# Two-layer transformer trunk on one core: the sum of squares at stage boundaries, the residual adds, and one compression weight move between engines

## The chip, the cores and the metric

The kernel runs on one core of a Trainium2 chip. The core has a matrix engine (TensorE, PE in the profile, with PEld for its weight loads), VectorE (DVE), ScalarE (ACT), GpSimd (POOL) and SyncE (SP, which here only issues DMAs); each works through its own instruction list in order and waits on semaphores for the others. The metric is the device time of one execution in microseconds.

## The reference

Two layers over 512 tokens of width 1024, in fp32. Cut to the stages:

```python
hn = rms_norm(x, norm_g[0])
parts = split_columns(hn @ w_in)                 # 8 NSA query heads, K/V x3, gates, 4 stick-breaking heads, 2 merge gates
kc = compress_blocks(k_c, cmp_pe[0], cmp_w1[0], cmp_w2[0])   # gelu(blocks @ w1) @ w2, for keys
vc = compress_blocks(v_c, cmp_pe[1], cmp_w1[1], cmp_w2[1])   # and for values
y_nsa = nsa_attention(...) @ w_nsa_o             # compressed + selected + window branches
y_sb  = stick_breaking_attention(...) @ w_sb_o
mixed = (gate_a * y_nsa + gate_b * y_sb) @ w_out
x = x + rms_norm(mixed, norm_g[1])               # boundary: post-norm, residual
hf = rms_norm(x, norm_g[2])                      #           and the next pre-norm
ff = square(relu(hf @ w_ff1)) @ w_ff2
x = x + rms_norm(ff, norm_g[3])                  # the second boundary of the layer
```

`rms_norm` divides each token by the root of the mean of its 1024 squares.

## The kernel before

Activations lie transposed, features on the 128 partitions and the 512 tokens along the free axis, so x is eight tiles x0 to x7 of 128 x 512, and a matmul of a 128 x 128 weight block moves 512 or 256 columns. Full fp32 precision comes from three matmuls in a fast fp32 format: operands are split into a high and a low part (`w_hi`, `w_lo` of a weight; `ah`, `al` of an activation), and `three` (L185 to L187) issues hi x hi, hi x lo, lo x hi.

**Weights.** The class `Weight` loads 128 x 1024 raw values into one of two buffers (tag `wr`), lets ACT copy them rounded into `w_hi` (L157), and then has POOL subtract for `w_lo` (L162). The raw buffer is free for the next load when that subtract is done. With `sub="dma"` it goes another way: ACT writes the rounded raw weight, negated, into `w_lo` (L159), and POOL issues a DMA that adds the raw weight from DRAM to it (L160); POOL then does no arithmetic on it. Which of the four first-layer weights (u = 0 to 3) of the two compressions use this is set by bits of `PLAN["CKM"]` (keys) and `PLAN["CVM"]` (values). `CKM` 2 means u = 1 of the keys.

**Boundaries.** `tail` is called four times, at the ends of `w_out` and of `w_ff2` in both layers. It handles the last five of the eight output tiles and the passage into the next stage; the last call has no next stage (`nxt` is None), so three of the four are boundaries as meant here: 1 (near 430 us), 2 (near 800) and 3 (near 1230). The 512 tokens are handled in two halves of 256. PE computes the five tiles of the first half, then those of the second. Each finished tile is copied out of PSUM by DVE (L261; at the end of `w_ff2` it is added to an earlier part, L263), ACT squares it and DVE adds the square to a running sum (`macc` after `w_out`, `facc` after `w_ff2`, L237). `rstd_fin` sums that over the partitions by a matmul with a matrix of ones (tile `ss`, L212) and forms the reciprocal root `Rpost`. `residual` then takes each of the eight tiles: `pn` = tile x gain x Rpost (DVE, L291), x = pn + x_old (POOL, L292), `ah` = rounded x times the next gain (ACT, L226), `al` = the rest (DVE, L227). PE meanwhile runs the next stage's first four column groups (`head_step`, tile `head`) over these: two k steps on the first half before the second half's `ss`, six after it, and then the second half.

**Order.** PE's list is written out by hand. The lists of the other engines are laid out by a scheduler that simulates the timeline when the kernel is built, so an edit in one place can move instructions in others. Small squares, the cosine and sine tables and `x_old` share six buffers (tag `sig`).

Of the kernel before, what the change touches and what calls it, by code (L numbers as in the profile page):

```python
# [11 lines left out]
AF = mybir.ActivationFunctionType  # L12
ALU = mybir.AluOpType
# [9 lines left out]
}  # L23
GN = 5
# [25 lines left out]
def layer_kernel(ctx, tc, xT, pos, gvec, tri, consts, smalls, w_in, w1, w_o, w_out, ff1, ff2, out):  # L50
    nc = tc.nc
    V, S, G, E = nc.vector, nc.scalar, nc.gpsimd, nc.tensor
# [9 lines left out]
    def big(tag, name, dt=F32):  # L62
        return sp.tile([P, T], dt, tag=tag, bufs=BUFS[tag], name=name)

    def half(name):
        return sp.tile([P, 256], F32, tag="sv", bufs=3, name=name)

    def psum(tag, name):
        return pp.tile([P, T], F32, tag=tag, bufs=2, name=name)
# [10 lines left out]
    x = [big("L", f"x{k}") for k in range(KT)]  # L80
# [8 lines left out]
    ones = cp.tile([P, P], F32, name="ones")  # L89
# [99 lines left out]
    def dense(ps, w, acts, k0=0):  # L189
        n = len(acts)  # L190
        for k in range(n):
            three(ps, w, k0 + k, acts[k], k == 0, k == n - 1)

    HALVES = (slice(0, 256), slice(256, 512))
    FULL = (slice(0, 512),)

    def cols(acts, c):
        return [(h[:, c], l[:, c]) for h, l in acts]

    def head_step(group, acts, c, ks):  # L200
        for k in ks:
            for ps, w in group:
                three(ps[:, c], w, k, (acts[k][0][:, c], acts[k][1][:, c]), k == 0, k == KT - 1)

    def gcol(l, n, k):
        c = (l * 4 + n) * KT + k
        return gv[:, c:c + 1]

    def rstd_fin(R, acc, c, more=None, tag="t"):
        n = c.stop - c.start  # L210
        ss = psum(tag, "ss")[:, 0:n]
        E.matmul(ss, ones, acc, start=True, stop=more is None)  # L212
        if more is not None:
            E.matmul(ss, ones, more, start=False, stop=True)
        v = half("var")
        y = R[:, c]
        S.activation(y, ss, AF.Ln, scale=1.0 / D, bias=eps_c)
        V.tensor_scalar(v, ss, 1.0 / D, EPS, ALU.mult, ALU.add)
        S.activation(y, y, AF.Exp, scale=-0.5)
        V.tensor_tensor(acc, y, y, ALU.mult)  # L220
        V.scalar_tensor_tensor(v, acc, -0.5, v, ALU.mult, ALU.mult)
        V.scalar_tensor_tensor(y, v, 1.5, y, ALU.add, ALU.mult)

    def xsplit(act, xk, g, c):
        h, l = act[0][:, c], act[1][:, c]
        S.activation(h, xk[:, c], AF.Copy, scale=g)  # L226
        V.scalar_tensor_tensor(l, xk[:, c], g, h.bitcast(F32), ALU.mult, ALU.subtract)  # L227

    def sq_add(acc, src, first, c, eng):
        n = c.stop - c.start  # L230
        if first:
            S.activation(acc, src, AF.Square)
        else:
            for o in range(0, n, 256):
                sq = sp.tile([P, 256], F32, tag="sq", bufs=2, name="sq")
                S.activation(sq, src[:, o:o + 256], AF.Square)
                eng.tensor_tensor(acc[:, o:o + 256], acc[:, o:o + 256], sq, ALU.add)  # L237

    def new_acts():
        return [(big("act", f"ah{k}", F32R), big("act", f"al{k}", F32R)) for k in range(KT)]  # L240

    def tail(l, n, mixed, acc, load, acts, prev, src, nxt, head):


        group = range(KT - GN, KT)
        last_sq = []
        na = new_acts() if nxt is not None else None
        R = big("R", "Rpost")
        R2 = big("R", "Rpre") if nxt is not None else None
        ws = [load(m, ("f", "w", "w", "w", "pt")[i]) for i, m in enumerate(group)]  # L250
        pst = [psum(("d", "s", "o", "o", "s")[i], f"tail{m}") for i, m in enumerate(group)]

        def products(hf, i):
            c = HALVES[hf]
            dense(pst[i][:, c], ws[i], cols(acts, c))

        def evacuate(hf, i):
            c = HALVES[hf]
            m, ps = group[i], pst[i][:, c]
            if prev is None:  # L260
                V.tensor_copy(mixed[m][:, c], ps)  # L261
            else:
                V.tensor_tensor(mixed[m][:, c], ps, prev[m][:, c], ALU.add)  # L263
            if nxt is None and (hf, i) == (1, GN - 1):
                last_sq.append(half("last_sq"))
                S.activation(last_sq[0], mixed[m][:, c], AF.Square)
            else:
                sq_add(acc[:, c], ps if prev is None else mixed[m][:, c], False, c, V)
            if nxt is None and hf == 1:
                S.activation(mixed[m][:, c], mixed[m][:, c], AF.Copy, scale=gcol(l, n, m))  # L270

        def old(hf):
            if src is None:
                return [x[k][:, HALVES[hf]] for k in range(KT)]
            r = []
            for j in range(4):
                t = big("sig", "x_old").rearrange("p (a t) -> p a t", a=2)
                nc.sync.dma_start(t, src[:, 2 * j:2 * j + 2, HALVES[hf]])
                r += [t[:, 0, :], t[:, 1, :]]
            return r  # L280

        def residual(hf, xo):
            c = HALVES[hf]
            for k in range(KT):
                t = big("t", "pn")[:, 0:256]
                if nxt is None and hf == 1:
                    e = G if k in ENDP else V
                    e.tensor_tensor(t, mixed[k][:, c], R[:, c], ALU.mult)
                    (G if k == 5 else e).tensor_tensor(x[k][:, c], t, xo[k], ALU.add)
                else:  # L290
                    V.scalar_tensor_tensor(t, mixed[k][:, c], gcol(l, n, k), R[:, c], ALU.mult, ALU.mult)  # L291
                    (V if nxt is None and k in (1, 4, 7) else G).tensor_tensor(x[k][:, c], t, xo[k], ALU.add)  # L292
                if nxt is not None:
                    xsplit(na[k], x[k], gcol(nxt[0], nxt[1], k), c)
                else:
                    nc.sync.dma_start(out[:, k, c], x[k][:, c])

        def squares(hf):
            c = HALVES[hf]
            acc2 = half("acc2")  # L300
            for k in range(KT):
                sq_add(acc2, x[k][:, c], k == 0, c, V)
            return acc2

        for i in range(GN):
            products(0, i)
            evacuate(0, i)
        xo = old(0)
        if src is not None:
            for k in range(KT):  # L310
                x[k] = big("L", f"x{k}")
        products(1, 0)
        rstd_fin(R, acc[:, HALVES[0]], HALVES[0])
        evacuate(1, 0)
        hd = head.start() if nxt is not None else None
        residual(0, xo)
        for i in range(1, GN):
            products(1, i)
            evacuate(1, i)
        xo = old(1)  # L320
        if nxt is None:
            for m in range(KT - GN):
                S.activation(mixed[m][:, HALVES[1]], mixed[m][:, HALVES[1]], AF.Copy, scale=gcol(l, n, m))
            rstd_fin(R, acc[:, HALVES[1]], HALVES[1], last_sq[0])
            residual(1, xo)
            return None
        head_step(hd, na, HALVES[0], (0, 1))
        rstd_fin(R, acc[:, HALVES[1]], HALVES[1])
        residual(1, xo)
        a2 = squares(0), squares(1)  # L330
        head_step(hd, na, HALVES[0], range(2, KT))
        head_step(hd, na, HALVES[1], range(PLAN["HS"]))
        rstd_fin(R2, a2[0], HALVES[0])
        head_step(hd, na, HALVES[1], range(PLAN["HS"], PLAN["HS2"]))
        rstd_fin(R2, a2[1], HALVES[1])
        head_step(hd, na, HALVES[1], range(PLAN["HS2"], KT))
        return na, R2, hd
# [118 lines left out]
    class Head:  # L456
# [5 lines left out]
        def load(self, sub=None, between=None):  # L462
            u = len(self.ws)
            self.ws.append(Weight(self.src[u], "P" if u < 3 else "w", sub, between))
# [549 lines left out]
    with tc.manual_schedule(engines={mybir.EngineType.PE}):  # L1014
        acts = new_acts()
        R = big("R", "R0")
        acc = big("st", "acc0")
# [16 lines left out]
        nxt = acts, R, hd  # L1034
        for l in range(DEPTH):
            nxt = layer(l, *nxt)
# [71 lines left out]
```

## Time and profile before

| | |
|---|---|
| three runs | 1608.31, 1613.12, 1613.18 us; median 1613.12 |
| profiled execution | 1610.72 us, span 1608.8 us |
| PE busy | 1528.3 us, 95% of the span |
| DVE, ACT, POOL busy | 858.1 (53%), 748.9 (47%), 763.2 us (47%) |
| POOL, the subtract L162 | 204 times, 2425 ns each |
| ACT, w_hi L157 | 226 times, 1059 ns each |
| raw weight loads | 3.5 to 3.7 us from issue to landing |

The profile is of one execution. A timeline row gives start and duration in us, engine, line, operation, output and inputs with the shape, how many in a row are put together (x), and in brackets how long the engine stood idle before and which engine's operation ended that. In a timeline the ends of matmuls are modelled; their starts tell the pace. PEclk is the granted clock of PE as a share of 2.4 GHz.

### The profile page before, as it was taken

The page shows a single profiled execution, that of the slowest core. Times are in us where ns is not written, and L with a number is a line of the kernel's source. Part 1 is how long each engine was busy: PE and PEld are TensorE (multiplying, and loading weights), DVE is VectorE, ACT ScalarE, POOL GpSimd, SP SyncE. Part 2 cuts the span into 40 slices and gives each one's busy share as a digit, 9 for nine tenths or more (in the row PEclk, how much of TensorE's full clock was granted, in tenths as well). Part 3 has the DMA queues.
Part 4 walks back from the last instruction along what each step waited for, and adds up shares of the span by engine and source line. Part 5 has one row for each costly group of instructions (what it writes and reads, how often), then busy time and mean ns, then how long its engine had stood idle before and what let it go on. Part 6 is the DMA issues. An engine that isn't in the chain of part 4 may idle for free.

```text
span 1608.8 us, 20693 instructions
## 1 busy us (share of the span) xinstructions
PE 1528.3 (95%) x7810; PEld 1288.8 (80%) x7810; DVE 858.1 (53%) x1495; ACT 748.9 (47%) x1379; POOL 763.2 (47%) x527
## 2 busy tenths in 40 slices
PE   7789999999989999999988899999998999999996
PEld 5667778887978888888976787788878988888886
DVE  6788854355583232314698887534447713232245
ACT  6567754553352322324446777554444523232342
POOL 4574344535544444446546724444464444444452
PEclk9899999999999999999999999999999999999998
DMA  6443312224313233233334512122342132323321
GB/s 195 121 131 92 64 55 77 66 91 145 105 43 104 93 94 103 92 102 121 117 100 131 136 49 66 53 79 71 113 144 92 47 98 92 105 92 97 100 92 53
DMA packets 49331, 153.74 MB, mean 96 GB/s; under 512 B 5952, under 2 KB 12496, under 8 KB 49232
## 3 DMA queue, kind: packets, MB, share of 16 engines
q1 hardware_dynamic: 45888, 140.84, 27.2%
q0 software_dynamic: 3200, 11.55, 4.1%
q8 instruction: 61, 1.00, 0.3%
q14 instruction: 38, 0.31, 0.1%
q10 hardware_dynamic: 144, 0.03, 0.0%
HBM read 148.15 MB, written 4.26 MB: 95 GB/s over the span
## 4 chain that ended last, share of the span: by engine, by line
PE 78%; DVE 12%; ACT 2%; issue 2%; DMA 1%; POOL 1%; DVEq 0%; ACTq 0%; POOLq 0%
PE ff L186 12%; PE ff L187 12%; PE ff L185 12%; PE proj L479 5%; PE proj L483 5%; PE proj L481 5%; PE tail L187 2%; PE tail L186 2%; PE tail L185 2%; PE y L185 2%; PE p_t L720 2%; DVE P L690 2%; PE y L186 2%; PE y L187 2%; DVE pn L291 2%
## 5 line engine op out<-in xcount | busy, mean ns | idle before, releaser
L162 POOL TENSOR_TENSOR w_lo<-w_raw,w_hi 128x1024 fp32r<-128x1024 f32 x204 | 494.6, 2425 | 506.1 <-ACT w_hi L157 493.6
L157 ACT ACTIVATE w_hi<-w_raw 128x1024 fp32r<-128x1024 f32 x226 | 239.1, 1059 | 521.2 <-PE ff L186 371.7
L483 PE MATMUL proj<-ah,w_lo 128*128 128x512 f32 x496 | 198.7, 401 | 1.7 <-POOL w_lo L162 1.7
L479 PE MATMUL proj<-ah,w_hi 128*128 128x512 f32 x496 | 199.2, 402 | 0.9 <-ACT w_hi L157 0.9
L481 PE MATMUL proj<-al,w_hi 128*128 128x512 f32 x496 | 198.9, 401 | 0.0
L185 PE MATMUL ff<-ah,w_hi 128*128 128x512 f32 x448 | 174.3, 389 | 0.0
L186 PE MATMUL ff<-al,w_hi 128*128 128x512 f32 x448 | 174.3, 389 | 0.0
L187 PE MATMUL ff<-ah,w_lo 128*128 128x512 f32 x448 | 174.3, 389 | 0.0
L186 PE MATMUL ff<-hl,w_hi 128*128 128x512 f32 x432 | 168.2, 389 | 0.7 <-DVE hl L181 0.7
L185 PE MATMUL ff<-hh,w_hi 128*128 128x512 f32 x432 | 168.1, 389 | 0.0
L187 PE MATMUL ff<-hh,w_lo 128*128 128x512 f32 x432 | 168.1, 389 | 0.0
L181 DVE TENSOR_TENSOR hl<-relu,hh 128x512 fp32r<-128x512 f32 x64 | 106.8, 1673 | 83.7 <-ACT hh L180 83.5
L483 PEld LDWEIGHTS proj<-ah,w_lo 128*128 128x128 f32 x496 | 94.8, 191 | 19.0 <-POOL w_lo L162 2.1
L479 PEld LDWEIGHTS proj<-ah,w_hi 128*128 128x128 f32 x496 | 95.0, 192 | 17.4 <-ACT w_hi L157 1.1
L481 PEld LDWEIGHTS proj<-al,w_hi 128*128 128x128 f32 x496 | 95.0, 192 | 16.7
L1003 DVE TENSOR_TENSOR ffa<-ff,ffa 128x512 f32<-128x512 f32 x38 | 26.3, 692 | 151.3 <-PE ff L187 151.3
L185 PEld LDWEIGHTS ff<-ah,w_hi 128*128 128x128 f32 x448 | 84.1, 188 | 17.5
L187 PEld LDWEIGHTS ff<-ah,w_lo 128*128 128x128 f32 x448 | 84.1, 188 | 17.3
L186 PEld LDWEIGHTS ff<-al,w_hi 128*128 128x128 f32 x448 | 84.1, 188 | 17.3
L186 PEld LDWEIGHTS ff<-hl,w_hi 128*128 128x128 f32 x432 | 81.1, 188 | 17.9 <-DVE hl L181 1.1
L185 PEld LDWEIGHTS ff<-hh,w_hi 128*128 128x128 f32 x432 | 81.1, 188 | 17.0
L187 PEld LDWEIGHTS ff<-hh,w_lo 128*128 128x128 f32 x432 | 81.1, 188 | 16.6
(311 smaller groups left out, 3401.3 us busy)
## 6 DMA issues: line engine op xcount, KB each, us to landing
w_raw<-in_ff_dram SPq DMA_DIRECT2D x128, 512.0 KB, 3.5
w_raw<-in_w_in_dram SPq DMA_DIRECT2D x69, 512.0 KB, 3.6
w_lo<-in_w_in_dram POOLq DMA_DIRECT2D x18, 512.0 KB, 7.7
w_raw<-in_w_dram SPq DMA_DIRECT2D x16, 512.0 KB, 3.6
w_raw<-in_w_o_dram SPq DMA_DIRECT2D x16, 512.0 KB, 3.5
w_raw<-in_w_out_dram SPq DMA_DIRECT2D x16, 512.0 KB, 3.7
x<-in_xT_dram SPq DMA_DIRECT2D x8, 256.0 KB, 6.8
w_lo<-in_w_dram POOLq DMA_DIRECT2D x4, 512.0 KB, 7.0
```

Of the source, the lines that this page charges most:

```text
L157: S.activation(h, raw, AF.Copy)
L162: (sub or G).tensor_tensor(l, raw, h.bitcast(F32), ALU.subtract)
L181: V.tensor_tensor(lo, src, hi.bitcast(F32), ALU.subtract)
L185: E.matmul(ps, w.hi(k), ah, start=first, stop=False)
L186: E.matmul(ps, w.hi(k), al, start=False, stop=False)
L187: return E.matmul(ps, w.lo(k), ah, start=False, stop=last)
L291: V.scalar_tensor_tensor(t, mixed[k][:, c], gcol(l, n, k), R[:, c], ALU.mult, ALU.mult)
L479: E.matmul(ps, w.hi(k), ah, start=(k == 0), stop=False)
L481: E.matmul(ps, w.hi(k), al, start=False, stop=False)
L483: E.matmul(ps, w.lo(k), ah, start=False, stop=(k == KT - 1))
L690: V.tensor_scalar(pr[h], pr[h], sm4[:, h:h + 1], None, ALU.mult)
L720: E.transpose(pt[:, P * h:P * h + P], pend[j][0][h][:, P * kt:P * kt + P], ident)
```

## The change

Three things are edited. In the three boundaries, the second half's five squares are written by ACT into tiles of their own (`sq2`, halves of three `sig` buffers), from PSUM or, at boundary 2, from the summed tile; DVE no longer adds them up, and `rstd_fin` passes them to PE, which adds five more ones-matmuls to the one over the running sum (L214, now in a loop). In `residual`, the adds x = pn + x_old at these boundaries, sixteen at each, are given to DVE where POOL did them. `CKM` becomes 0, so the low part of the keys' u = 1 weight is made by POOL's subtract as for the other weights. Lines of the changed kernel from `tail` on are numbered five higher.

```diff
--- before.py
+++ after.py
@@ -18,7 +18,7 @@
     "GE": 7, "GA": 1, "GB": 4,
     "F0": 76, "F2": 5, "F3": 1, "F1": 7, "AH": 7, "BU": 2, "QD": 77, "FS0": 4, "FS1": 4, "FE": 5, "FN00": 5, "FN01": 3, "FN02": 4,
     "FN03": 7, "FN10": 6, "FN11": 4, "FN12": 4, "FN13": 7, "FNC0": 1, "FNC1": 7, "CK0": 11, "CK1": 24, "CK2": 13,
-    "CK3": 36, "CV0": 13, "CV1": 28, "SC3": 1, "SC2": 2, "R1": 3, "R2": 4, "CKV": 1, "CKM": 2, "CVM": 1, "ORD": 2, "HS": 6, "H0": 2, "HS2": 7, "FQ": 12,
+    "CK3": 36, "CV0": 13, "CV1": 28, "SC3": 1, "SC2": 2, "R1": 3, "R2": 4, "CKV": 1, "CKM": 0, "CVM": 1, "ORD": 2, "HS": 6, "H0": 2, "HS2": 7, "FQ": 12,
     "CD": 0, "GT": 24,
 }
 GN = 5
@@ -210,8 +210,8 @@
         n = c.stop - c.start
         ss = psum(tag, "ss")[:, 0:n]
         E.matmul(ss, ones, acc, start=True, stop=more is None)
-        if more is not None:
-            E.matmul(ss, ones, more, start=False, stop=True)
+        for i, m in enumerate(more or ()):
+            E.matmul(ss, ones, m, start=False, stop=i == len(more) - 1)
         v = half("var")
         y = R[:, c]
         S.activation(y, ss, AF.Ln, scale=1.0 / D, bias=eps_c)
@@ -243,7 +243,7 @@
 
 
         group = range(KT - GN, KT)
-        last_sq = []
+        last_sq, pairs = [], []
         na = new_acts() if nxt is not None else None
         R = big("R", "Rpost")
         R2 = big("R", "Rpre") if nxt is not None else None
@@ -264,6 +264,11 @@
             if nxt is None and (hf, i) == (1, GN - 1):
                 last_sq.append(half("last_sq"))
                 S.activation(last_sq[0], mixed[m][:, c], AF.Square)
+            elif nxt is not None and hf == 1:
+                if i % 2 == 0:
+                    pairs.append(big("sig", "sq2"))
+                last_sq.append(pairs[-1][:, 256 * (i % 2) : 256 * (i % 2) + 256])
+                S.activation(last_sq[-1], ps if prev is None else mixed[m][:, c], AF.Square)
             else:
                 sq_add(acc[:, c], ps if prev is None else mixed[m][:, c], False, c, V)
             if nxt is None and hf == 1:
@@ -289,7 +294,7 @@
                     (G if k == 5 else e).tensor_tensor(x[k][:, c], t, xo[k], ALU.add)
                 else:
                     V.scalar_tensor_tensor(t, mixed[k][:, c], gcol(l, n, k), R[:, c], ALU.mult, ALU.mult)
-                    (V if nxt is None and k in (1, 4, 7) else G).tensor_tensor(x[k][:, c], t, xo[k], ALU.add)
+                    (G if nxt is None and k not in (1, 4, 7) else V).tensor_tensor(x[k][:, c], t, xo[k], ALU.add)
                 if nxt is not None:
                     xsplit(na[k], x[k], gcol(nxt[0], nxt[1], k), c)
                 else:
@@ -321,11 +326,11 @@
         if nxt is None:
             for m in range(KT - GN):
                 S.activation(mixed[m][:, HALVES[1]], mixed[m][:, HALVES[1]], AF.Copy, scale=gcol(l, n, m))
-            rstd_fin(R, acc[:, HALVES[1]], HALVES[1], last_sq[0])
+            rstd_fin(R, acc[:, HALVES[1]], HALVES[1], last_sq)
             residual(1, xo)
             return None
         head_step(hd, na, HALVES[0], (0, 1))
-        rstd_fin(R, acc[:, HALVES[1]], HALVES[1])
+        rstd_fin(R, acc[:, HALVES[1]], HALVES[1], last_sq)
         residual(1, xo)
         a2 = squares(0), squares(1)
         head_step(hd, na, HALVES[0], range(2, KT))
```

The order of DVE at boundary 1 shows the first two edits. Before, from the first half's Rpost on (`pn`, `al` with their tile numbers; `mix` is a tile of the stage's output, `macc` the running sum):

```order
L291 SCALAR_TENSOR_TENSOR pn_4177<-mix0_3765,gv_67,Rpost_3929 128x256
L291 SCALAR_TENSOR_TENSOR pn_4182<-mix1_3766,gv_67,Rpost_3929 128x256
L291 SCALAR_TENSOR_TENSOR pn_4187<-mix2_3767,gv_67,Rpost_3929 128x256
L291 SCALAR_TENSOR_TENSOR pn_4192<-mix3_3768,gv_67,Rpost_3929 128x256
L237 TENSOR_TENSOR macc_3773<-macc_3773,sq_4242 128x256
L291 SCALAR_TENSOR_TENSOR pn_4197<-mix4_3769,gv_67,Rpost_3929 128x256
L227 SCALAR_TENSOR_TENSOR al0_3914<-x0_4122,gv_67,ah0_3913 128x256
L261 COPY mix5_3770<-tail5_3971 128x256
L237 TENSOR_TENSOR macc_3773<-macc_3773,sq_4270 128x256
L291 SCALAR_TENSOR_TENSOR pn_4202<-mix5_3770,gv_67,Rpost_3929 128x256
L261 COPY mix6_3771<-tail6_3972 128x256
L227 SCALAR_TENSOR_TENSOR al1_3916<-x1_4123,gv_67,ah1_3915 128x256
```

And in the changed kernel, from the same place, where `x0` to `x5` are the adds now on DVE:

```order
L296 SCALAR_TENSOR_TENSOR pn_4175<-mix0_3764,gv_67,Rpost_3928 128x256
L296 SCALAR_TENSOR_TENSOR pn_4180<-mix1_3765,gv_67,Rpost_3928 128x256
L296 SCALAR_TENSOR_TENSOR pn_4185<-mix2_3766,gv_67,Rpost_3928 128x256
L296 SCALAR_TENSOR_TENSOR pn_4190<-mix3_3767,gv_67,Rpost_3928 128x256
L261 COPY mix4_3768<-tail4_3969 128x256
L297 TENSOR_TENSOR x0_4121<-pn_4175,x_old_4113 128x256
L297 TENSOR_TENSOR x1_4122<-pn_4180,x_old_4113 128x256
L297 TENSOR_TENSOR x2_4123<-pn_4185,x_old_4115 128x256
L297 TENSOR_TENSOR x3_4124<-pn_4190,x_old_4115 128x256
L296 SCALAR_TENSOR_TENSOR pn_4195<-mix4_3768,gv_67,Rpost_3928 128x256
L261 COPY mix5_3769<-tail5_3970 128x256
L296 SCALAR_TENSOR_TENSOR pn_4200<-mix5_3769,gv_67,Rpost_3928 128x256
```

The two adds into macc are gone from this stretch, four x adds stand behind the first four pn, and al0 stands behind pn5; al1 follows six rows later (al0, pn6, pn7, x4, x5, al1).

On ACT at boundary 1, the second half's last squares in the changed kernel (`sq2`, read from the PSUM tiles `tail6` and `tail7`):

```order
L226 ACTIVATE ah4_3920<-x4_4125,gv_67 128x256
L271 ACTIVATE sq2_4266<-tail6_3971 128x256
L226 ACTIVATE ah5_3922<-x5_4126,gv_67 128x256
L226 ACTIVATE ah6_3924<-x6_4127,gv_67 128x256
L226 ACTIVATE ah7_3926<-x7_4128,gv_67 128x256
L271 ACTIVATE sq2_4319<-tail7_3972 128x256
L217 ACTIVATE Rpost_3928<-ss_4353,eps_c_78 128x256
```

The last of the five squares stands behind ah7 and right ahead of Rpost's first step.

On ACT in layer 1 (q and K rows of the sparse attention; the `w_hi` here is that of the next projection), before:

```order
L571 ACTIVATE qph_7509<-q_7495 128x512
L531 ACTIVATE K1w_7444<-kr_7469 64x512 x2
L533 ACTIVATE K2s_7445<-K2s_7445 64x512
L157 ACTIVATE w_hi_7636<-w_raw_7634 128x1024
L350 ACTIVATE xr10_7503<-qr_7497 64x512
L350 ACTIVATE xr11_7506<-qr_7497 64x512
L543 ACTIVATE V20_7447<-v_t_7513 128x4x64
```

and in the changed kernel:

```order
L576 ACTIVATE qph_7504<-q_7490 128x512
L536 ACTIVATE K1w_7439<-kr_7464 64x512 x2
L538 ACTIVATE K2s_7440<-K2s_7440 64x512
L355 ACTIVATE xr10_7498<-qr_7492 64x512
L355 ACTIVATE xr11_7501<-qr_7492 64x512
L548 ACTIVATE V20_7442<-v_t_7508 128x4x64
L157 ACTIVATE w_hi_7630<-w_raw_7628 128x1024
```

The w_hi has moved behind the two xr and a V. On POOL, the subtract for the keys' u = 1 weight stands in layer 0 exactly where the DMA stood, between `qr` and `qpl`; in layer 1 it stands ahead of `qr` and the block splits `bhl`, where the DMA stood behind `qr`.

## Rows read from the trace of the kernel before

**Rows 1.** Waits of PE: engine, line, what ended them; us in total, times, longest.
```profile
PE ss L212 <- DVE macc L237: 8.2, 2, 4.1
...
PE ss L212 <- DVE facc L237: 5.7, 2, 5.0
```

**Rows 2.** Timeline of PE, boundary 1: start, us, operation [wait before it <-releaser].
```profile
428.83 0.60 PE L212 MATMUL ss<-macc,ones 128*128 128x256 f32 x2
...
429.38 0.28 PE L186 MATMUL tail<-ml,w_hi 128*128 128x256 f32 x1
...
444.39 0.39 PE L186 MATMUL head<-al,w_hi 128*128 128x256 f32 x1 [1.90 <-DVE al L227]
...
450.08 1.22 PE L212 MATMUL ss<-macc,ones 128*128 128x256 f32 x2 [4.12 <-DVE macc L237]
```

**Rows 3.** Windows behind the sums: length; busy us of PE, PEld, DVE, ACT, POOL; PEclk; DMA.
```profile
450.10:453.60 3.50, 3.50 (x14) 3.32 (x15) 2.63 (x7) 2.83 (x8) 0.24 (x1) 0.50 0.60 191
453.70:458.00 4.30, 4.30 (x38) 4.30 (x38) 4.30 (x9) 2.32 (x6) 2.78 (x4) 1.00 0.01 1
809.70:815.40 5.70, 5.70 (x25) 5.52 (x26) 5.16 (x13) 3.41 (x10) 0.95 (x2) 0.50 0.15 57
```

**Rows 4.** Timeline of PE, boundary 2.
```profile
809.66 1.22 PE L212 MATMUL ss<-facc,ones 128*128 128x256 f32 x2 [4.95 <-DVE facc L237]
```

**Rows 5.** Timeline of DVE, boundary 1.
```profile
431.56 0.43 DVE L222 SCALAR_TENSOR_TENSOR Rpost<-var,Rpost 128x256 f32<-128x256 f32 x1
...
447.14 0.41 DVE L261 COPY mix<-tail 128x256 f32<-128x256 f32 x1
447.47 2.23 DVE L227 SCALAR_TENSOR_TENSOR al<-x,gv,ah 128x256 fp32r<-128x256 f32 x1
449.62 0.41 DVE L237 TENSOR_TENSOR macc<-macc,sq 128x256 f32<-128x256 f32 x1
```

**Rows 6.** Timeline of POOL, boundary 1.
```profile
436.66 3.55 POOL L292 TENSOR_TENSOR x<-pn,x_old 128x256 f32<-128x256 f32 x4
...
446.89 2.52 POOL L162 TENSOR_TENSOR w_lo<-w_raw,w_hi 128x1024 fp32r<-128x1024 f32 x1
```

**Rows 7.** Timeline of PE, compression of keys in layer 0.
```profile
67.71 0.47 PE L379 MATMUL cmp_h<-w_lo,bhl 128*64 128x256 f32 x1 [8.83 <-DMA w_lo<-in_w_dram]
```

**Rows 8.** Windows from the next w_lo to cmp_o, layers 0 and 1 (columns as in 3).
```profile
63.24:96.21 32.97, 22.43 (x107) 18.00 (x108) 22.36 (x43) 19.25 (x38) 23.72 (x14) 0.86 0.51 141
858.03:890.55 32.52, 24.78 (x100) 19.22 (x100) 27.33 (x44) 21.09 (x42) 24.09 (x14) 0.84 0.44 129
```

**Rows 9.** Timeline of PE, the same stretch of layer 1.
```profile
860.45 0.80 PE L483 MATMUL proj<-ah,w_lo 128*128 128x512 f32 x1 [1.71 <-POOL w_lo L162]
...
890.55 0.64 PE L409 MATMUL cmp_o<-cmp_ht,sml 128*64 128x32 f32 x4 [2.89 <-DVE cmp_ht L400]
```

**Rows 10.** Timeline of ACT, layer 0.
```profile
57.20 1.06 ACT L157 ACTIVATE w_hi<-w_raw 128x1024 fp32r<-128x1024 f32 x1
...
60.40 1.28 ACT L350 ACTIVATE xr<-qr 64x512 fp32r<-64x512 f32 x2
...
62.11 1.06 ACT L157 ACTIVATE w_hi<-w_raw 128x1024 fp32r<-128x1024 f32 x1
```

**Rows 11.** Timeline of POOL, layer 0.
```profile
60.09 1.58 POOL L143 TENSOR_TENSOR qpl<-q,qph 128x512 fp32r<-128x512 f32 x1
```

**Rows 12.** Timeline of DVE, layer 0.
```profile
46.11 3.88 DVE L344 TENSOR_TENSOR rope_sh<-rope_sh,sinT 128x512 f32<-128x512 f32 x1
...
58.82 0.69 DVE L344 TENSOR_TENSOR rope_sh<-rope_sh,sinT 128x512 f32<-128x512 f32 x1
```

**Rows 13.** Timeline of ACT, layer 1.
```profile
844.46 1.04 ACT L157 ACTIVATE w_hi<-w_raw 128x1024 fp32r<-128x1024 f32 x1
...
856.90 1.06 ACT L157 ACTIVATE w_hi<-w_raw 128x1024 fp32r<-128x1024 f32 x1
```

**Rows 14.** Timeline of POOL, layer 1.
```profile
849.94 0.86 POOL L160 DMA_DIRECT2D w_lo<-in_w_dram  x1
```

## Prediction

> **What bounds the kernel now.** I read first the busy shares: TensorE (PE) works for 95% of the span, so an edit counts only where PE stands still or runs at half clock, or where it gives PE more to do. Next I read the waits of PE, sorted by what ended them. The two groups that the title aims at stand there: PE waits for the last sum of squares at the first and third stage boundary (together 8.2 us, two times, 4.1 at the longest) and at the second (5.0 of a group of 5.7) [rows 1]. Then the timeline of PE at boundary 1: after the first two k steps of the next stage it waits 1.90 us for an al, and the matmul ss comes 4.12 us late [rows 2]. The windows show what the wait costs beyond itself: over the 3.5 us behind it the granted clock is 0.50, so 1.2 GHz, and only 14 matmuls run, where the 4.3 us after that hold 38 at 1.00 (2.4 GHz); at boundary 2 the half-clock stretch is 5.7 us [rows 3], behind a wait of 4.95 [rows 4]. PE had stood idle before both.
>
> Why is the sum late? DVE's rows at boundary 1: its last copy out of PSUM starts at 447.14 and the last add of squares at 449.62 [rows 5], while PE had its tail products done before 442.5, the start of its 1.90 us wait [rows 2]. Between the two DVE rows lies one al of 2.23 us, where a VectorE operation on 256 columns otherwise takes 0.41 to 0.43 [rows 5]: POOL's subtract of 1024 columns runs at that moment, 446.89 for 2.52 us [rows 6]. Such a subtract holds DVE for its whole length. Four x adds on POOL take 3.55 us [rows 6], twice what DVE would need.
>
> The third place is the compression of keys in layer 0: PE waits 8.83 us for a w_lo that comes by DMA [rows 7]. It looks like the largest single prize.
>
> **The change, part by part.**
>
> *Squares to PE.* Five 256-column ones-matmuls per boundary are added, fifteen in all. One costs 0.43 us at full clock: ss starts at 428.83, and the second product behind it starts at 429.38, 0.12 after the first one would [rows 2]. That is 15 x 0.43 = 6.4 us more for PE. In return the fifteen DVE adds go, and the ones-matmuls wait on ACT alone. In ACT's order the last square stands behind ah7, though, so it still waits for the last x.
>
> *The x adds to DVE* (48, which the title does not name). At boundary 1, from the end of Rpost at 432.0 [rows 5] to al1 DVE now has 18 instructions (pn0 to pn3, a copy, x0 to x3, pn4, a copy, pn5, al0, pn6, pn7, x4, x5, al1). Their starts lie 0.33 (the copy at 447.14 and the al behind it [rows 5]) to 0.43 (a whole duration) apart, some 6.7 us. Three POOL subtracts fall in this stretch; one is 2.52 us [rows 6], and I count 6.8 in all, since a little of each falls beside a copy, which reads PSUM. al1 is then there at about 445.5, against the 444.39 of now [rows 2]: the first wait grows from 1.9 to about 3. Eleven head products of 0.12 (38 take 4.3 [rows 3]) bring PE to 446.8, six ones-matmuls of 0.43 to 449.4. The last square is in time for it: x6, al2, x7 on DVE, ah7 and the square on ACT, about 2 us behind al1. Today ss ends near 451.2 (450.08 and the 1.22 of its row [rows 2], less the modelled end). So the sum comes 1.8 us earlier. Whether the half-clock stretch goes as well is open: the trace shows it behind 4.12 us, and no row has a single wait of 3. The stretch costs half of 3.5 us, 1.75. So boundary 1 gains between 0.8 (the half clock now lies on the head products and ones-matmuls) and 3.5; I take 2.2, the middle, and the same at boundary 3, whose wait repeats this one (two times [rows 1]).
>
> At boundary 2 there is no al wait today. The sum starts at 809.66 [rows 4]; after, it needs only the square of the last tile, which DVE must still add to ffa first. DVE's chain up to there loses five adds of 0.41 (as at 449.62 [rows 5]) and its waits for POOL's x adds of 0.9 each (four in 3.55 [rows 6]), and gains eight adds of about 0.35: I put the last square 2.2 us earlier, between 0.4 (only the add behind it goes) and 3. With the ones-matmul at full clock, 0.43 for 1.0, the sum ends some 2.8 us earlier. The half-clock stretch of 5.7 us [rows 3], 2.8 us of cost, may shrink, for PE then stands still for under 3 us instead of 4.95. Gain 1 to 5; I take 4.0, in the upper half for want of an al wait. Together the boundaries give 2.2 + 2.2 + 4.0 = 8.4 us, with the 6.4 us of new matmuls inside. The second half's chain on DVE takes about 8 us from the sum to its first al (2.5 for Rpost, then some 15 instructions at 0.33 to 0.43), and PE has six k steps of 12 products at 0.12, 8.6 us, to cover it; if that cover fails, the excess comes back at each boundary.
>
> *Keys' weight part to POOL, layer 0.* PE's 8.83 us wait goes: the subtract needs w_hi, which ends at 58.26 [rows 10], so w_lo is there at about 60.7 instead of 67.7. I do not credit PE with this. From the subtract of the next weight (63.24) to the matmul cmp_o the stretch takes 32.97 us in layer 0 and 32.52 in layer 1, with PE busy for only 22.4 and 24.8 of it [rows 8]. In layer 1 there is no such DMA wait: PE's third product of the next projection starts 2.4 us behind that subtract (860.45 against 858.03 [rows 9]), in layer 0 it starts after 67.71 [rows 7], over 4 us behind. Both take equally long, so what sets the length is the chain of raw load, w_hi and w_lo through two raw buffers, and PE only has to be there. The question is then what moves the start of this chain, the w_hi at 62.11. It stands on ACT behind the two xr from 60.40 [rows 10], and these wait for DVE's rope (the product with the sine table at 58.82 [rows 12] and an add). The new subtract lies on POOL from 58.3 to 60.7, just over that product. The bounds: if DVE gets in when the subtract ends, the rope is late by about 1.5 us; if POOL's next one, qpl of 1.58 [rows 11], holds DVE too, by 2.9. A row for the second: a product of DVE that began at 46.11 took 3.88 us, through three POOL operations in a row [rows 12]. I take 2.2 us later. What covers the rest today, a DMA that needs no SBUF input of DVE's, is gone.
>
> The Trainium skill ("SBUF — State Buffer", section "Who interferes with whom") says that the shared port pair goes to whichever of the two issues first, and that the other blocks for that one instruction. By that rule DVE gets in after the subtract, the 1.5 of the lower bound. The row at 46.11 speaks for more than one instruction.
>
> *Layer 1.* There the subtract needs the w_hi from 844.46, which ends at 845.5 [rows 13], and holds DVE's first rope chain until 847.9, up to 2.4 us; the DMA's issue on POOL goes (0.86 [rows 14], of which I count 0.6, since neighbours overlap). In ACT's order the next w_hi, at 856.90 today directly behind K2s [rows 13], now stands behind two xr and a V, 1.6 us. So 2.2 + 1.6 - 0.6 = 3.2 us later; between 1.0 (DVE not held) and 3.6. Both layers: 2.2 + 3.2 = 5.4 us lost.
>
> *Rest.* SP issues the second half's x_old loads later, behind a raw load that waits for the second POOL subtract, and DVE needs them only some 7 us after the sum; layer 1's cosine tables are loaded a boundary later. I cost both at nothing: the six k steps above hide the first, the whole of boundary 2 the second.
>
> Sum: -8.4 + 5.4 = -3.0 us against the profiled execution's 1610.7 (span 1608.8, and 1.9 around it that the change leaves alone), so 1607.7. The runs shown have a median of 1613.1, 2.4 above it, with one at 1608.3; I put the forecast at 1608.
>
> **Rivals.**
>
> A. *The 8.8 us wait simply goes.* Then PE is the bound in layer 0, and the 6.9 us by which w_lo comes earlier are gained without a loss on DVE: -8.4 - 6.9 = -15.3, 1595. For it: it is PE's longest wait behind a DMA [rows 7] and PE is 95% busy overall. Against it: the equal lengths of [rows 8].
>
> B. *DVE gets in between POOL's operations*: 1.5 and 1.0 instead of 2.2 and 3.2. -8.4 + 2.5 = -5.9, 1605. For it: the al at 447.47 was held for just one subtract [rows 5, 6]. Against it: the 3.88 at 46.11.
>
> C. *POOL holds the chain that DVE now carries*, slower. With the x adds on DVE, every POOL subtract that falls between al1 and the last x also delays ah7, the last square and the sum. If one more, 2.4 us, falls there at each boundary, these give 8.4 - 7.2 = 1.2, and the same holding puts the two layers at their far ends, 2.9 + 3.6 = 6.5: +5.3, 1616. It decides from the point at which the last square comes after PE's five others. For it: DVE's al at 447.47. Against it: today's third subtract already falls there and I have counted three.
>
> **How the numbers follow.** Forecast 0.50, A 0.17, B 0.16, C 0.12; 0.05 for none of them. The forecast's own range is -8 to +1 us, 1603 to 1612. A measurement of this kernel tells about 0.3%, 4.8 us, from no change. Faster by more: all of A, two thirds of B, 0.3 of the forecast: 0.17 + 0.11 + 0.15 = 0.43. Slower by more: most of C and a little of the rest, 0.13. Within: 0.44. The range goes up to C and down to the edge of A: 1596 to 1616.
>
> **What would show it.** Right: ss at the three boundaries starts without a wait for macc or facc; a wait for al of about 3 us at boundaries 1 and 3; no cmp_h wait in layer 0, but w_hi of the next projection there at about 64 instead of 62.1, and cmp_o 2 us later; the stretch to cmp_o still 32 to 33 us long. Wrong: cmp_o of layer 0 earlier than 94 (A); rope's sine product ending before 62 in layer 0 (B); a wait of ss for the last square above 1 us (C).

## The result, and the profile after

The changed kernel takes 1602.35 us (median of four runs, 1601.39 to 1604.44) against 1612.82 for the kernel before on the same chip. The ratio is 0.9949 with a 95% interval of 0.993 to 0.9968, so 8.2 us faster, between 5.2 and 11.3 (the two medians alone lie 10.5 apart; this document goes by the recorded ratio). The time lies in the range (1596 to 1616) and the direction was forecast, but the likeliest value, 1608, was 5.7 us too high, and 1602.35 lies just outside the forecast's own 1603 to 1612. The profiled execution has a span of 1600.6 us, 8.2 below that of before.

The waits of PE first (engine, line, what ended them; us in total, times, longest), as the answer to [rows 1] and [rows 7]:

```profile
PE cmp_o L414 <- issue: 9.6, 2, 5.1
...
PE head L186 <- DVE al L227: 5.5, 4, 2.4
...
PE cmp_h L384 <- POOL w_lo L162: 1.9, 1, 1.9
...
PE ss L212 <- DVE facc L237: 0.7, 1, 0.7
```

The waits of ss for macc are gone, and of the two for facc the one of 5.0 is gone; the 0.7 that stay are at the fourth `tail`, which the change leaves alone. What is left of the keys' wait for its low part is 1.9. The waits for al have grown from 4.6 to 5.5 in all, and cmp_o waits twice about 5 us where one of 4.8 and one of 2.9 stood.

PE's timeline at boundary 1 and, after the dots, at boundary 2, beside [rows 2, 4]:

```profile
444.66 0.39 PE L186 MATMUL head<-al,w_hi 128*128 128x256 f32 x1 [2.38 <-DVE al L227]
...
446.07 0.96 PE L212 MATMUL ss<-macc,ones 128*128 128x256 f32 x2
446.82 3.69 PE L214 MATMUL ss<-sq,ones 128*128 128x256 f32 x10
...
802.75 0.60 PE L212 MATMUL ss<-facc,ones 128*128 128x256 f32 x2
803.18 2.32 PE L214 MATMUL ss<-sq,ones 128*128 128x256 f32 x10
```

The wait for al is 2.38 us; ss follows at 446.07 with no wait and its ten further records (five matmuls) behind it. At boundary 2 neither stands.

What DVE does ahead of al1, beside [rows 5]:

```profile
437.54 2.60 DVE L296 SCALAR_TENSOR_TENSOR pn<-mix,gv,Rpost 128x256 f32<-128x256 f32 x1
...
440.46 3.08 DVE L296 SCALAR_TENSOR_TENSOR pn<-mix,gv,Rpost 128x256 f32<-128x256 f32 x2
...
444.14 0.47 DVE L227 SCALAR_TENSOR_TENSOR al<-x,gv,ah 128x256 fp32r<-128x256 f32 x1
```

A pn takes 2.60 us and the next two 3.08 together, where a pn alone takes 0.47: each time a POOL subtract holds DVE (the third, from 440.48 for 2.38 us, has moved up beside the second). The al at 444.14 is al1.

The windows (columns as in [rows 3]):

```profile
446.80:450.60 3.80, 3.80 (x14) 3.14 (x13) 1.51 (x4) 0.43 (x2) 0.00 (x0) 0.63 0.73 219
450.60:454.00 3.40, 3.40 (x31) 3.40 (x30) 2.92 (x9) 2.34 (x6) 0.00 (x0) 1.00 0.19 64
...
805.60:812.00 6.40, 6.40 (x56) 6.40 (x55) 6.40 (x19) 3.70 (x11) 0.00 (x0) 1.00 0.29 97
...
65.42:97.99 32.57, 23.52 (x101) 18.17 (x101) 22.66 (x42) 18.96 (x38) 24.09 (x14) 0.87 0.44 130
852.86:885.49 32.63, 22.67 (x101) 17.30 (x101) 24.19 (x42) 19.51 (x39) 25.55 (x15) 0.87 0.45 131
```

At boundary 1 the granted clock is still down (0.63 over the six ones-matmuls: part at 1.2 GHz, the rest at 2.4), at boundary 2 it no longer falls. The last two are the stretches of [rows 8], from the next subtract to cmp_o: 32.57 and 32.63 us, where 32.97 and 32.52 stood. Of PE's 8.83 us wait 4.5 lay in the first of them (63.24 to 67.71); that wait is gone, one of 3.76 us for DVE (ahead of 65.84) stands there instead, and the stretch is 0.4 us shorter.

To see where the 8.2 us came from I follow the same matmul through both traces:

| place | before, us | after, us | difference | gained since the row above |
|---|---|---|---|---|
| cmp_o, layer 0 | 96.21 | 97.99 | +1.78 | -1.78 |
| attention's output, last column group | 384.14 | 385.29 | +1.15 | +0.63 |
| ten us later | 394.56 | 394.29 | -0.27 | +1.42 |
| first ss of boundary 1 | 428.83 | 428.56 | -0.27 | 0 |
| next norm's ss of boundary 1 | 469.49 | 467.62 | -1.87 | +1.60 |
| first ss of boundary 2 | 789.73 | 787.93 | -1.80 | -0.07 |
| next norm's ss of boundary 2 | 830.03 | 822.61 | -7.42 | +5.62 |
| cmp_o, layer 1 | 890.55 | 885.49 | -5.06 | -2.36 |
| first ss of boundary 3 | 1220.66 | 1214.21 | -6.45 | +1.39 |
| next norm's ss of boundary 3 | 1261.34 | 1253.20 | -8.14 | +1.69 |

The boundaries give 1.6 + 5.6 + 1.7 = 8.9 us (forecast 8.4). The layers lose 1.8 and 2.4 us up to cmp_o (forecast 2.2 and 3.2), but most of that comes back behind cmp_o, and there the forecast had nothing. In layer 0 the largest part, 1.42 us, comes back within ten us at 384 to 394, in code that the change doesn't touch.

Layer 0 itself, DVE, ACT, POOL and PE, beside [rows 7, 10 to 12]:

```profile
58.46 2.41 DVE L349 TENSOR_TENSOR rope_sh<-rope_sh,sinT 128x512 f32<-128x512 f32 x1
60.97 1.57 DVE L350 TENSOR_TENSOR qr<-qr,rope_sh 128x512 f32<-128x512 f32 x1
```
```profile
62.58 1.28 ACT L355 ACTIVATE xr<-qr 64x512 fp32r<-64x512 f32 x2 [3.52 <-DVE qr L350]
...
64.29 1.06 ACT L157 ACTIVATE w_hi<-w_raw 128x1024 fp32r<-128x1024 f32 x1
```
```profile
57.96 2.35 POOL L162 TENSOR_TENSOR w_lo<-w_raw,w_hi 128x1024 fp32r<-128x1024 f32 x1 [0.87 <-ACT w_hi L157]
60.27 1.72 POOL L143 TENSOR_TENSOR qpl<-q,qph 128x512 fp32r<-128x512 f32 x1
```
```profile
60.37 0.43 PE L384 MATMUL cmp_h<-w_lo,bhl 128*64 128x256 f32 x1 [1.86 <-POOL w_lo L162]
...
97.99 0.59 PE L414 MATMUL cmp_o<-cmp_ht,sml 128*64 128x32 f32 x4 [4.47 <-issue]
```

POOL's subtract holds the sine product from 58.46 to 60.87 (2.41 for 0.69), qpl then holds the add that follows it (1.57 for 0.69), the xr start at 62.58 instead of 60.40, w_hi at 64.29 instead of 62.11, and PE, which now has its low part at 60.37, ends at a cmp_o 1.78 us later. The Trainium skill ("SBUF — State Buffer", section "Who interferes with whom") lets the engine that issues second wait out one instruction of the other; these two rows agree, each DVE operation was held by one POOL operation and got in before the next had ended.

Layer 1 has one such product; the first row is of the kernel before, the other two, of DVE and ACT, of the changed kernel:

```profile
845.74 0.68 DVE L344 TENSOR_TENSOR rope_sh<-rope_sh,sinT 128x512 f32<-128x512 f32 x1
```
```profile
838.39 2.88 DVE L349 TENSOR_TENSOR rope_sh<-rope_sh,sinT 128x512 f32<-128x512 f32 x1
```
```profile
851.73 1.06 ACT L157 ACTIVATE w_hi<-w_raw 128x1024 fp32r<-128x1024 f32 x1
```

The subtract there (838.27 to 840.72) holds it for 2.2 us. The next w_hi stood at 856.90 [rows 13]; less the 7.42 us gained up to there that is 849.48, so it comes 2.25 us later, and cmp_o 2.36.

### The profile page after: what moved, and what is told of

The parts are those of the page before. It is cut to its first block, busy times and chain, and to the rows that moved or that the text cites. A ratio compares the mean times of both kernels' runs of the same rounds, so it can differ in the third digit from the quotient of the medians.

```text
span 1600.6 us, 20731 instructions
## 1 busy us (share of the span) xinstructions
PE 1530.1 (96%) x7840; PEld 1289.7 (81%) x7840; DVE 849.1 (53%) x1528; ACT 744.6 (47%) x1377; POOL 727.3 (45%) x479
## 4 chain that ended last, share of the span: by engine, by line
PE 79%; DVE 10%; issue 2%; ACT 2%; DMA 2%; POOL 2%; DVEq 0%; ACTq 0%; POOLq 0%
PE ff L186 12%; PE ff L185 12%; PE ff L187 12%; PE proj L484 5%; PE proj L488 5%; PE proj L486 5%; PE tail L185 2%; PE tail L187 2%; PE tail L186 2%; PE p_t L725 2%; DVE P L695 1%; PE y L185 1%; PE head L186 1%; PE y L186 1%; PE head L187 1%
## 5 line engine op out<-in xcount | busy, mean ns | idle before, releaser
L185 PEld LDWEIGHTS ff<-hh,w_hi 128*128 128x128 f32 x432 | 81.1, 188 | 16.7
```

The lines of the kernel that those rows point to most:

```text
L185: E.matmul(ps, w.hi(k), ah, start=first, stop=False)
```

## The experiments

Theory 1: the squares on PE make the gain; the keys' subtract on POOL costs about 2 us per layer through DVE; what came back behind cmp_o came back because half-clock stretches happened to fall otherwise. Rivals: the 8.8 us wait was worth something (2); what lies behind absorbs any delay (3). Differences in us are the ratio's, with its interval, from the kernel before on the same chip.

**The weight part put back** (edit on the changed kernel):

```diff
-    ... "CKM": 0, ...
+    ... "CKM": 2, ...
```

> The changed kernel with the keys' u = 1 weight part back on the DMA; squares and x adds stay as changed. Theory 1 (the POOL subtract costs about 2 us per layer up to cmp_o, and what came back of it afterwards came back only because the half-clock stretches fell differently): boundaries as in the changed kernel, cmp_h waits 8 us again, and the time is 1 to 4 us below the changed kernel's, so 9 to 12 below before. Theory 2 (rival A, the 8.8 us wait was worth something): 4 to 7 us above the changed kernel. Theory 3 (the stretch behind absorbs either): within 1 us of the changed kernel.

1598.09 us, ratio 0.9935 (0.9916 to 0.9954): 10.5 us below before (7.4 to 13.5), and 4.3 below the changed kernel by the medians, which are of two chips. Theory 2 falls. The time is what theory 1 expected, but the intervals of the two ratios overlap, so that only the next run excludes theory 3. One thing is not as in the changed kernel, PE at boundary 3:

```profile
1227.01 0.39 PE L186 MATMUL head<-al,w_hi 128*128 128x256 f32 x1 [2.38 <-DVE al L227]
...
1228.43 0.60 PE L212 MATMUL ss<-macc,ones 128*128 128x256 f32 x2
1228.86 2.32 PE L214 MATMUL ss<-sq,ones 128*128 128x256 f32 x10
```

The wait for al is the same 2.38 us, but the granted clock stays at 1.00 behind it, where in the changed kernel, and at boundary 1 of this one, it falls to 0.50.

**The weight part alone** (the same edit the other way, on the kernel before):

> The kernel before with only the keys' u = 1 weight part moved to POOL. Theory 1: slower than before by 1 to 4 us, cmp_o late by 2 us in both layers. Theory 2: faster by 4 to 7. Theory 3: within 1 us.

1615.58 us, ratio 1.0034 (1.0023 to 1.0046): 5.5 us slower (3.7 to 7.4), more than the 1 to 4 that I gave theory 1 here, and as much as the prediction's sum for the two layers, 5.4. PE and ACT of layer 0 in its trace:

```profile
60.62 0.33 PE L379 MATMUL cmp_h<-w_lo,bhl 128*64 128x256 f32 x1 [1.82 <-POOL w_lo L162]
...
98.06 0.60 PE L409 MATMUL cmp_o<-cmp_ht,sml 128*64 128x32 f32 x4 [4.48 <-issue]
```
```profile
64.54 1.06 ACT L157 ACTIVATE w_hi<-w_raw 128x1024 fp32r<-128x1024 f32 x1
```

PE's wait at the low part is 1.82 instead of 8.83 us, w_hi comes 2.43 us later, cmp_o 1.85 later, and the matmul of 388.06 us is still 2.05 later, at 390.11: nothing has come back. From the next norm's ss of boundary 2 to cmp_o of layer 1 it takes 62.74 us where 60.52 stood, 2.2 more. Another 1.6 of the 5.8 us between the two spans come behind that cmp_o, where the clock is at 0.50 from about 1186 to 1190 us. The kernel before has no such stretch there in its profile, but the x adds alone and the subtract on DVE (both below) have it too, with the weight part by DMA or on DVE; so these 1.6 us are not the subtract's on POOL.

**The squares alone** (on the kernel before; the loop in `rstd_fin` and the `sq2` tiles as in the change):

```diff
+            elif nxt is not None and hf == 1:
+                ...
+                S.activation(last_sq[-1], ps if prev is None else mixed[m][:, c], AF.Square)
```

> The kernel before with only the squares given to PE; x adds on POOL, weight part by DMA. If the squares alone remove the waits for macc and facc (theory 1), ss starts without a wait at all three boundaries, 1.9 us for al stay, and the time is 5 to 8 us below before. If the x adds on DVE are what makes the last squares early enough (rival), ss still waits 2 us or more for the last square behind ah7 and the time is 0 to 3 us below before.

1594.06 us, ratio 0.9907 (0.989 to 0.9924): 15.0 us faster (12.2 to 17.7), twice what I expected, and faster than the whole change. PE at boundary 1, and the windows of what follows there:

```profile
441.23 0.60 PE L212 MATMUL ss<-macc,ones 128*128 128x256 f32 x2
441.66 1.89 PE L214 MATMUL ss<-sq,ones 128*128 128x256 f32 x8
443.71 0.70 PE L214 MATMUL ss<-sq,ones 128*128 128x256 f32 x2 [0.16 <-ACT sq L271]
```
```profile
444.40:450.00 5.60, 5.60 (x50) 5.60 (x48) 5.60 (x13) 2.52 (x8) 1.70 (x3) 1.00 0.49 161
```

With the x adds on POOL, al1 is there before PE asks, ss starts at 441.23, and the last square, which in this order stands ahead of ah6 and ah7, costs 0.16 us. PE stands still for nothing that lowers the clock: 1.00 behind the sum, and the same at the other two boundaries.

**The x adds alone** (on the kernel before):

```diff
-(V if nxt is None and k in (1, 4, 7) else G).tensor_tensor(x[k][:, c], t, xo[k], ALU.add)
+(G if nxt is None and k not in (1, 4, 7) else V).tensor_tensor(x[k][:, c], t, xo[k], ALU.add)
```

> The kernel before with only the 48 x adds moved to DVE; the squares are still added up by DVE. Theory 1: DVE trades POOL's hold for adds of its own, the wait of ss for macc and facc stays at 3 to 5 us, and the time is within 2 us of before. Rival: freed of POOL's adds DVE ends the sums 2 us earlier at each boundary, and the time is 4 to 7 us below before.

1610.7 us, ratio 1.0006 (0.9995 to 1.0017): 1.0 us slower (0.8 faster to 2.7 slower). PE at boundary 1:

```profile
442.90 0.39 PE L186 MATMUL head<-al,w_hi 128*128 128x256 f32 x1 [0.22 <-DVE al L227]
...
449.79 1.22 PE L212 MATMUL ss<-macc,ones 128*128 128x256 f32 x2 [5.31 <-DVE macc L237]
```

The al wait is short and ss waits 5.31 us instead of 4.12, but the sum is not later: this ss starts 21.13 us behind the first one of the boundary (428.66), where 21.25 stood [rows 2]. The wait has moved from al to ss, and no difference can be told in the time.

**Squares, with the second half's x adds on DVE and the first half's on POOL:**

```diff
+(V if (nxt is None and k in (1, 4, 7)) or (nxt is not None and hf == 1) else G).tensor_tensor(x[k][:, c], t, xo[k], ALU.add)
```

> Squares on PE and the weight part by DMA, as in the squares-only kernel, but the x adds of the second half (24 of 48) on DVE, those of the first half on POOL. Theory (the x adds on DVE cost because in the first half they stand ahead of al1 and of the last square, nothing in the second): no al wait in the first half, ss starts as in the squares-only kernel, the al waits of the second half (0.6 us at boundaries 1 and 3) go, and the time is 0 to 2 us below the squares-only kernel's, 15 to 18 below before. Rival (any x add on DVE costs): 2 us above the squares-only kernel.

1593.63 us, ratio 0.9891 (0.9876 to 0.9906), 17.6 us faster. Since that is another chip, both were run again side by side:

> The squares-only kernel once more, beside the next on one chip. Theory as before (15 us below the kernel before, none of the half-clock stretches at the three boundaries). If its first profile owed the missing stretch at 388 us to chance, it may be there now, 1.7 us, and the boundaries stay as they were.

> Squares on PE, second half's x adds on DVE, once more beside the squares-only kernel. If those adds cost nothing there and take the short al waits of the second half away, 0.5 to 3 us below the squares-only kernel; if they cost, above it.

1594.88 and 1594.82 us, ratios 0.9894 (0.9879 to 0.9909) and 0.9892 (0.9876 to 0.9909): no difference. The waits for al fall by about 1.1 us in all (3.0 to 1.9), too little to tell. So it is the first half's x adds on DVE that cost, not the second half's (boundary by boundary below), and these two are the fastest versions seen, about 17 us below the kernel before.

**Squares and the weight part on POOL, x adds on POOL:**

> Squares on PE and the keys' weight part on POOL; x adds stay on POOL. If the parts add up (squares -15, weight part +4 to +5.5), 10 to 11 us below before, and so below the changed kernel. If the weight part's cost hangs on how the half-clock stretches fall, anything from 10 to 15 below.

1600.32 us, ratio 0.9928 (0.9911 to 0.9944): 11.6 us faster (9.0 to 14.3). The parts add up within their intervals.

**The changed kernel again, unaltered:**

> The changed kernel once more, unaltered, for a second profile. If the half-clock stretches fall by chance from execution to execution, their places or lengths differ from the first profile (84 to 88, 98 to 102, 446 to 450, 852 to 860, 883 to 890 and 1231 to 1235 us, and none at 388) and the time of each stretch with it. If they belong to the kernel, they are the same, with none at 388. Time 8 to 10 us below before.

1603.37 us, ratio 0.995 (0.9935 to 0.9965). Its span is 1602.4, 1.8 more than in the first profile, and the same matmul runs 0.30 us later than there until 388 us and 1.95 later from 394 on. The windows of that place, in the kernel before, in the first profile of the changed kernel and in the second (columns as in [rows 3]):

```profile
389.00:392.00 3.00, 3.00 (x9) 2.33 (x8) 1.93 (x2) 1.58 (x2) 0.76 (x2) 0.50 0.60 193
```
```profile
390.50:393.50 3.00, 3.00 (x15) 2.50 (x14) 2.30 (x3) 1.58 (x2) 0.76 (x2) 1.00 0.60 187
```
```profile
390.50:393.50 3.00, 3.00 (x9) 2.37 (x8) 2.14 (x2) 1.52 (x2) 0.90 (x1) 0.55 0.53 178
```

Behind a wait of PE that all have, PE runs at 0.50 before, at 1.00 in the first profile and at 0.55 in the second: 9, 15 and 9 matmuls in three us. So the 1.42 us of the table above are a draw, not the change's. The way from cmp_o of layer 0 to the first ss of boundary 1 shows the same in all twelve profiles: 330.1 to 330.9 us in the five without half clock near 390 us, 332.5 to 333.6 in the seven with it, whatever the edit.

**The same subtract on DVE** (on the kernel before):

```diff
-sub="dma" if ... else None
+sub=V if (self.i, u) == (0, 1) else "dma" if ... else None
```

> The kernel before with the keys' u = 1 subtract on DVE instead of POOL or DMA, for what the hold of DVE costs. One such subtract should take DVE about 1.4 us. If DVE's delay sets the loss, the next w_hi of layer 0 comes 1.3 to 1.5 us later than before and cmp_o as much (2.1 with the subtract on POOL), and the time is 1 to 4 us above before. If POOL's place in the order sets it, cmp_o is not later than before and the time is within 1 us of it or below.

1611.28 us, ratio 0.9995 (0.9986 to 1.0004): no difference that can be told, where 1 to 4 us more were expected. DVE, ACT and PE of layer 0:

```profile
58.01 1.21 DVE L162 TENSOR_TENSOR w_lo<-w_raw,w_hi 128x1024 fp32r<-128x1024 f32 x1
59.14 1.78 DVE L344 TENSOR_TENSOR rope_sh<-rope_sh,sinT 128x512 f32<-128x512 f32 x1
```
```profile
63.46 1.06 ACT L157 ACTIVATE w_hi<-w_raw 128x1024 fp32r<-128x1024 f32 x1
```
```profile
59.28 0.33 PE L379 MATMUL cmp_h<-w_lo,bhl 128*64 128x256 f32 x1 [1.01 <-DVE w_lo L162]
...
97.00 0.63 PE L409 MATMUL cmp_o<-cmp_ht,sml 128*64 128x32 f32 x4 [4.42 <-DVE cmp_ht L400]
```

The subtract takes DVE 1.21 us, qpl holds the sine product for another 1.1, w_hi comes at 63.46 (+1.35) and cmp_o at 97.00 (+0.79; +1.4 against the rows ahead of this place, which lie 0.6 earlier in this execution). PE's wait is 1.01 us and again buys nothing in layer 0. In layer 1 cmp_o is 0.83 us earlier (889.72), which I have not followed up; with that the loss is made good.

## Why the prediction was right or wrong

*Squares.* "The sum comes 1.8 us earlier" held in direction; at boundary 1 its last product ended near 450.5 instead of 451.3, so 0.8 earlier, because the half clock now lay on the ones-matmuls themselves. The ones-matmuls cost what was reckoned where the clock stood at 1.00 (0.43 us from the first to the second at 802.75). At boundary 1 the wait for al was put at about 3 us and al1 at 445.5; they were 2.38 and 444.66. The last square was in time, as forecast. At boundaries 1 and 3 the gain of 2.2 each was 1.6 and 1.7, at boundary 2 4.0 was 5.6, since there the clock did not fall at all. The sum of 8.4 agrees with the 8.9 of the profile and with the 10.5 (7.4 to 13.5) of the run without the weight part, but in part by luck: two terms were 0.5 to 0.6 too high, and the third was 1.6 too low and above the top of its own 1 to 5.

*The x adds* were counted inside that sum and never priced alone. This was the blind spot: squares alone gain 15 us or more, so the adds on DVE take back some 4 us of it (0.9935 against 0.9907; the intervals overlap, but on that one chip every run of the squares alone was below every run of the other, 1595.73 against 1597.43). The length of each boundary, from its first ss to the next norm's ss, shows where:

| profile | boundary 1, us | boundary 2, us | boundary 3, us |
|---|---|---|---|
| before | 40.66 | 40.30 | 40.68 |
| x adds alone | 40.56 | 40.34 | 40.87 |
| squares alone | 36.17 | 35.98 | 36.18 |
| squares alone, again | 36.21 | 35.98 | 36.17 |
| squares, second half's x adds, again | 35.62 | 35.39 | 35.64 |
| changed kernel | 39.06 | 34.68 | 38.99 |
| changed kernel, again | 39.03 | 34.68 | 38.90 |
| changed kernel, weight part put back | 39.06 | 34.68 | 37.38 |

Alone the x adds change nothing that can be told. With the squares on PE they cost 2.9 us at boundary 1 and 2.8 at 3, and they gain 1.3 at boundary 2, where the changed kernel has no wait of PE left and the squares alone still have short ones for al in the second half (0.39 us the longest). At boundaries 1 and 3 they stand, in the first half, ahead of al1 among POOL's subtracts; that leaves the wait of 2.4 us, and behind it, in five of the six cases seen, a half-clock stretch that the squares alone don't have. The sixth (37.38) puts that stretch at 1.6 of the 2.9 us. So the adds of the first half should stay on POOL at boundaries 1 and 3; a kernel with them on DVE at boundary 2 alone was not run.

*Weight part.* The step "I do not credit PE with this" was right: PE lost a wait of 7 us there and cmp_o came later, in every kernel that had the subtract on POOL. The mechanism was right too, and in layer 0 so was its price up to cmp_o (2.2 forecast, 1.8 to 2.2 measured, by whether the 0.37 us by which the profile runs ahead at 45 us is counted). In layer 1 it was 3.2 forecast and 2.4 measured; the upper bound written there, 3.6, is 3.4 by its own terms (2.4 + 1.6 - 0.6). That the two layers together cost 5.5 when it is the only edit, against 5.4, is in part luck, since 1.6 of the 5.5 lay elsewhere. Rival A is refuted: cmp_o of layer 0 came at 97.99, not before 94. Of rival B the premise came true and the price did not. Its sign, the sine product ending before 62, was seen (60.87): DVE did get in between POOL's operations. But the add behind the product was then held by the next one, qpl, so that layer 0 still lost more than B's 1.5. Rival C's sign, a wait of ss for the last square of more than 1 us, was not seen.

*What failed* is the term of the sum that charged the change with 5.4 us for the layers: in the changed kernel's profile only 1.1 arrive at the boundaries behind them. Up to cmp_o 2.15 and 2.36 were lost (counting the 0.37 by which this profile ran ahead at 45 us), 0.9 less than forecast; then 0.63 + 1.42 and 1.39 came back. The 1.42 is a draw of the clock; with the second profile's 388 us the 1.1 would be 2.7. The 1.39 of layer 1 is no return of the subtract's loss either: from cmp_o of layer 1 to boundary 3 it takes 330.11 us before and 328.72 in the changed kernel, but also 328.79 with the squares alone (again) and 329.16 with the weight part put back, neither of which has the subtract on POOL. What shortens that way is not known. By the parts run alone, -10.5 + 5.5 = -5.0 us, just past the interval's upper end; the changed kernel measures 3 us better than that in both of its sets of runs (8.2 and 8.1 us below before). Half of that is the 1.6 us stretch at 1186 us, if the profile of the weight part alone stands for its runs; the rest lies within the intervals and is not settled.

*The range* held, but 1602.35 lies in it only because it was drawn down to the edge of rival A, which the runs refute; the forecast's own 1603 to 1612 missed by 0.65. That is luck, not a sign that the sum was right.

*The clock* was in the forecast only at the boundaries. As an estimate, if I add, over windows of 1 us, PE's busy share times what the granted clock lacks to 1.00, the kernel before loses 19.2 us, the changed kernel 14.3 (14.8 in its second profile), the squares alone 8.9 (8.1 in the second), the weight part alone 23.4. Of the 8.2 us between the two profiled executions 4.9 are clock by this count (3.1 at the boundaries, 1.7 near 390 us), of the 16.7 for the squares alone 10.3. The count also takes in half clock where PE has time to spare, as in the stretches to cmp_o, so it may overstate what the clock cost. The forecast had 1.75 to 2.8 us of it at a boundary and none elsewhere.

## What to carry to other kernels

A wait on the critical engine can cost a slow stretch behind it besides its length, so taking out all of a boundary's waits is worth more than taking out the longest: at boundary 1 the change took out the one of 4.12 us, left one of 2.4 and gained 1.6; the squares alone left none there above 0.2 ahead of the sum and gained 4.5. A long wait inside a stretch that another chain sets is worth nothing: compare the length of two stretches, one with and one without it, before crediting it. Where a change moves several things, price each one alone and place by place; here one of three made nearly all the gain, and the other two took back about half of it, though one of them helped at one boundary of three. And one profile of a kernel is one draw: take a second before explaining a difference of 1 or 2 us.

## What the runs showed of the hardware

The half clock behind the same wait is there in one execution and missing in the next. All twelve profiles have a wait of 2.3 to 3.2 us ahead of 390 us, seven of them have half clock behind it, and its length does not decide: 2.35 us had it, 3.00 had not. Of the three kernels that were profiled twice two (the changed one, and the one with the second half's x adds on DVE) have it once and not the other time, and it costs 1.4 to 1.7 us. Even within one execution, of the changed kernel with the weight part put back, a wait of 2.35 us at boundary 1 had it and one of 2.38 at boundary 3 had not. That may be much of the spread of some 5 us among runs of one kernel. Chance is perhaps not all of it: of the five profiles with squares on PE and the weight part by DMA four lack the stretch near 390 us, of the other seven one, and no run says why. The Trainium skill ("TensorE: Matmul & The Clock Gate", section "Part 1: The HAM clock gate") says that the chip's look at PE's activity runs on its own and does not start with the kernel. The two pairs of profiles would fit that, but no run here shows it.

POOL's subtract of 128 x 1024 (2.35 to 2.45 us) held DVE operations with two inputs in SBUF to its end, as shown above: a sine product of 0.69 us took 2.41, one of 0.68 took 2.88, a pn of 0.47 took 2.60. On DVE the same subtract took 1.21 us.
